# Gate and scale vectors of an output projection: other tiles, another queue, another order

## The chip, the cores and the metric

One core of a Trainium2 chip runs the whole program. The metric is the device time of one execution in microseconds. TensorE (PE) multiplies, with its own weight loads (PEld); VectorE (DVE), ScalarE (ACT) and GpSimd (POOL) do the elementwise work; SyncE (SP) issues nearly all DMAs. Each engine works through its own instructions in order.

## The reference

Two layers over 256 tokens `x` and 256 context tokens `xc`, model width 1024, float32. What matters here is the end of a layer's first half and the router that follows:

```python
merged = sigmoid(ga) * (y_a @ w_pa) + sigmoid(gb) * (y_b @ w_pb)
x = x + gt1 * (merged @ w_out)                    # gate gt1 per column
h2 = modulate(rmsnorm(x, g_ffn), sh2, sc2)        # h * (1 + sc2) + sh2
g_logits = h2 @ w_group + b_group                 # 4 groups
e_logits = h2 @ w_erouter + b_erouter             # 32 experts
# top group, top 2 experts in it, then per expert
y = (silu(h2 @ w1[e]) * (h2 @ w3[e])) @ w2[e]     # weighted, summed per token
x = x + gt2 * y
```

`gt1`, `sh2`, `sc2`, `gt2` are slices of 1024 columns of a vector of 6 * 1024 that the conditioning gives for each stream. The first layer updates both streams (512 tokens); the second, which is the last, updates only `x` (256 tokens).

## The kernel before

Each layer is a fixed order of stages: the input projections, spatial gating and retention, two projections that are merged, the output projection with the residual, the router, and 32 experts with 64 slots each. Matrix products outside the experts are made in three passes (`mm3`, lines 267 to 269) of high and low parts; `split_w` makes the parts of a weight piece on ACT (L209, `whi`) and DVE (L210, `wlo`).

**Weights.** `plan` lists the pieces of 512 KB in the order of use. `take` (L303) hands out the next and first fills a list of three with `fill`, so each piece is loaded two takes ahead. There are three buffers each for raw, high and low parts. `take` also calls `pump`, which loads expert weights ahead, in a ring of u4, a4, raw and high and low tiles. All these loads stand in SP's one queue in the order in which they are written; a load whose tile is not free holds up all behind it.

**Pools.** u4 has 30 tiles and a4 has 7, of 4 KB per partition; t2 has 7 of 2 KB. A new tile takes a buffer that its last readers have left. In the first layer, a4 also holds the vector that is being made for the next layer (`ada_steps`: raw tiles and an accumulator, read last by the matmuls of L448); in both it holds some weights of the first expert or two.

**Output projection.** `tok_wide` makes the first 512 columns for all token tiles (four in the first layer, two in the second) in four weight pieces of 256 rows. Then `residual(0)` and `residual(1)` follow for quarters of 256 columns: DVE multiplies by the gate (L980) and adds to the residual (L982), a third product with the scale gives `h2` (L984: POOL for the first three quarters, DVE for the last), and ACT squares for the norm (L986). `tok_major` makes the third quarter in two pieces, `(2, 0)` and `(2, 1)`, and `residual(2)` follows; `out_tile` makes the last quarter tile by tile, with `residual(3)` for each.

**Gate and scale vectors.** `mod_slices` loads, for a quarter and for each stream, both vectors to all partitions (256 KB into a t2 tile, L543). The first two quarters' slices are loaded on SP with weight pieces 2 and 3 (numbered from 0) of `tok_wide`, those of the last quarter with its second piece. Those of the third quarter are loaded by POOL's queue, in the program behind `residual(1)`.

**Router.** `route_piece(pc)` transposes `h2` of a quarter on PE (L993), ACT copies the result out of PSUM (L996), and a second step, `logits` (L1002), multiplies it by the router's weights. `defer(n, f)` puts `f` at the n-th next `tick`; `tok_major` has two ticks, one after each piece, and `flush()`, after `residual(2)`, runs what is left. So before, the transposes of piece 0 stand at the first tick, its logits at the second, and the transposes of piece 1, asked for at a third, run in `flush()`. The order of what follows is written out by hand (L1083): in `"o0 r o1 R t0 o2 ..."`, `o` is an `out_tile`, `r` the logits of piece 1 and the transposes of piece 2, `R` the logits of piece 2, `t` and `l` transposes and logits of the last quarter of a tile.

PE and SP run in program order throughout; from the second merging projection on, DVE, ACT and POOL do too.

Of the kernel before, what the change touches and what calls it, by code (L numbers as in the profile page):

```python
# [17 lines left out]
ALU = mybir.AluOpType  # L18
# [3 lines left out]
P = 128  # L22
# [32 lines left out]
def hybrid_kernel(  # L55
# [6 lines left out]
    nc = tc.nc  # L62
    depth = w_in.shape[0]
    V, S, G, T = nc.vector, nc.scalar, nc.gpsimd, nc.tensor
# [23 lines left out]
    def a4t(shape=(P, D), dt=F32):  # L88
        return a4.tile(list(shape), dt, tag="a4", name=nm("a4"))
# [45 lines left out]
    ada_d = [dr.tile([2, 6 * D], F32, name=f"ada{l}") for l in range(depth)]  # L135
# [89 lines left out]
    def defer(n, fn):  # L225
        deferred.append((ticks[0] + n, fn))
        deferred.sort(key=lambda d: d[0])
# [308 lines left out]

    ms = {}

    def mod_slices(l, pc, eng=None):
        r = []  # L540
        for i in range(1 if l == depth - 1 else 2):
            tl = t2t((P, 2, 256))
            (eng or nc.sync).dma_start(tl, ada_d[l][i].rearrange("(v n) -> v n", v=6)[2:5:2, pc * 256:(pc + 1) * 256].partition_broadcast(P))  # L543
            r.append(tl)
        return r

    def out_piece(l, pc, kh):
        r = piece(w_out[l], pc * 256, kh)
        if kh and pc == 3:
            ms[l, pc] = mod_slices(l, pc)  # L550
        return r

    def out_wide(l, q):
        r = piece_wide(w_out[l], 0, q)
        if q > 1:
            ms[l, q - 2] = mod_slices(l, q - 2)
        return r

    def plan(l):
# [15 lines left out]
    for l in range(depth):  # L575
        last = l == depth - 1
        layer[0], taken[0] = l, 0
        units.clear()
        nt = 2 if last else 4
# [117 lines left out]
        else:  # L697
# [9 lines left out]
            os_ = [bank() for _ in range(KD // 2)]  # L707
# [3 lines left out]
            for kp in range(KD // 2):  # L711
                if kp % 2 == 0:
                    tl = u4t((P, 4, NX))
# [40 lines left out]
        for g in range(2) if last else (1, 0):  # L754
            if last:
                os_, _ = tok_wide(tw)
            else:
                os_ = vo if g else [bank() for _ in tw]
# [3 lines left out]
                if not g:  # L762
                    for t in range(nt):
                        V.tensor_tensor(out=first[t], in0=os_[t], in1=first[t], op=ALU.add)
                    os_ = first
# [25 lines left out]
        for pc in range(4):  # L791
            os_, _ = feat_major(fj)
# [23 lines left out]
        for pc in range(4):  # L816
# [4 lines left out]
            os_, _ = feat_major(fj)  # L821
# [5 lines left out]
            os_, _ = feat_major([(f, yT, 0, nq) for f in range(2)])  # L827
            for f in range(2):
                if len(mg) * nq % 1024 == 0:
                    mgt = u4t((P, 1024 // nq, nq))  # L830
                m = mgt[:, len(mg) % (1024 // nq)]
# [6 lines left out]
        for h in range(HEADS):  # L838
# [10 lines left out]
            os_, _ = feat_major(qkj)  # L849
            qk = []  # L850
            for i in range(2):
                n = nq if i == 0 else NTOK
                o = os_[i]
                r = t2t()
# [60 lines left out]
            os_, _ = tok_wide(vgj)  # L915
# [9 lines left out]
        for pc in range(4):  # L925
            os_, gate_a_ = feat_major(fj)
# [16 lines left out]
        for pc in range(4):  # L943
            os_, gate_b = feat_major([(f, yT, 0, nq) for f in range(2)])
            m = [t2t() for _ in range(2)]
# [10 lines left out]
        res = []  # L956
# [10 lines left out]
        h2 = [u4t() for _ in range(nt)]  # L967
# [9 lines left out]
        def residual(pc, ts, os_, ms):  # L977
            cs = slice(pc * 256, (pc + 1) * 256)
            for t, o in zip(ts, os_):
                V.tensor_tensor(out=o, in0=o, in1=ms[t // 2][:, 0], op=ALU.mult)  # L980
            for t, o in zip(ts, os_):
                V.tensor_tensor(out=res[t][:, cs], in0=res[t][:, cs], in1=o, op=ALU.add)  # L982
            for t, o in zip(ts, os_):
                (G if pc < 3 else V).tensor_tensor(out=h2[t][:, cs], in0=res[t][:, cs], in1=ms[t // 2][:, 1], op=ALU.mult)  # L984
            for t, o in zip(ts, os_):
                S.activation(o, res[t][:, cs], AF.Square, accum_out=ssq[:, t, pc:pc + 1])  # L986

# [17 lines left out]
        def route_piece(pc):  # L1005
            rs_ = [turned(pc, (2 * i, 2 * i + 1)) for i in range(ns)]

            def rest():
                o = bank()
                for i in range(ns):  # L1010
                    logits(pc, (2 * i, 2 * i + 1), rs_[i], o)
                ov, lv = o[:, 0:nt * 36], lr[:, 0:nt].rearrange("p t e -> p (t e)")
                if pc == 0:
                    V.tensor_copy(lv, ov)
                else:
                    V.tensor_tensor(out=lv, in0=lv, in1=ov, op=ALU.add)

            return rest

        os_, _ = tok_wide([(mT[t // 2], t % 2 * P, 512) for t in range(nt)])  # L1020
        for pc in range(2):
            residual(pc, range(nt), [o[:, pc * 256:(pc + 1) * 256] for o in os_], ms[l, pc])
        ms[l, 2] = mod_slices(l, 2, G)
        waiting = []
        defer(1, lambda: waiting.append(route_piece(0)))
        defer(2, lambda: waiting.pop(0)())
        defer(3, lambda: waiting.append(route_piece(1)))
        os_, _ = tok_major([(mT[t // 2], t % 2 * P) for t in range(nt)])
        residual(2, range(nt), os_, ms[l, 2])
        wts = [take() for _ in range(2)]  # L1030
# [1 line left out]
        for i in range(ns):  # L1032
            tl = u4t()
# [49 lines left out]
        for op in ("o0 r o1 R t0 o2 l0 t1 s0 O3 l2 t3 s1 l3" if nt == 4 else "o0 r t0 o1 R l0 t1 l1").split():  # L1083
            t = int(op[1]) if op[1:] else None
# [20 lines left out]
        if split:  # L1105
            for t in range(nt):
# [7 lines left out]
                        in1=rc[:, 0:ns, None, :].to_broadcast([P, ns, 2, 36]), op=ALU.add)  # L1114
# [8 lines left out]
        for t in range(nt):  # L1123
# [5 lines left out]
                        in1=gf.to_broadcast([P, nt, GROUPS]), op=ALU.is_equal)  # L1129
# [3 lines left out]
                        in0=lo[:, 0:nt, 0:32].rearrange("p t (g e) -> p t g e", g=GROUPS),  # L1133
                        in1=goh[:, :, :, None].to_broadcast([P, nt, GROUPS, PER_GROUP]), op=ALU.add)
# [529 lines left out]
```

## Time and profile before

| | us |
|---|---|
| median of 3 runs | 1857.84 (1856.88 to 1861.28) |
| profiled execution | 1858.8 |
| its span, first to last instruction | 1857.0 |
| PE busy | 1798.0 (97%) |
| DVE busy | 916.7 (49%) |
| ACT busy | 590.9 (32%) |
| POOL busy | 386.3 (21%) |
| output projection and router, first layer | about 478 to 561 |
| experts, first layer | about 561 to 1047 |
| output projection and router, second layer | about 1332 to 1378 |
| experts, second layer | about 1378 to 1844 |

Times in the profile are microseconds from the start of the span. A row of the timeline gives start, length, engine, line, operation, names of output and inputs, and in brackets how long the engine sat idle before it and what released it. Rows of one kind that follow each other are merged, and their number stands at the end. A row of a table by stretch gives, per engine, busy time with the number of instructions, then the granted clock of TensorE as a share of 2.4 GHz, the share of the DMA engines' time, and GB/s.

### The profile page before, as it was taken

How to read it: one execution, taken by the hardware profiler on the slowest of the kernel's cores; microseconds unless marked ns; L12 is line 12 of the kernel's file. 1: busy time of each engine (PE TensorE's matmuls, PEld its weight loads, DVE VectorE, ACT ScalarE, POOL GpSimd, SP SyncE). 2: the span in 40 equal slices, each digit the busy share in tenths (PEclk: the TensorE clock that was granted, in tenths of full speed). 3: DMA queues.
4: the chain of work that ended last, by engine and by line, in shares of the span. 5: the costliest groups of instructions: out<-in, count | busy, mean ns of one | idle time of the engine just before them, and what ended most of it. 6: DMA issues, size and time to landing. Idle time of an engine off the chain costs nothing. (4 is left out here: it accounts for less than half of the span.)

```text
span 1857.0 us, 26227 instructions
## 1 busy us (share of the span) xinstructions
PE 1798.0 (97%) x9975; PEld 1190.8 (64%) x9975; DVE 916.7 (49%) x1582; ACT 590.9 (32%) x979; POOL 386.3 (21%) x351
## 2 busy tenths in 40 slices
PE   7999999999969999999999899999989999999996
PEld 4888888888865444454544489999964444444442
DVE  4878886664544323333332577767633222222223
ACT  4432345432332222121212364454432222221222
POOL 1021022100130424232323340211021212112111
PEclk9999999999979999999999999999989999999998
DMA  9546544454568999999999569656789999999996
GB/s 346 179 144 226 183 137 125 147 205 167 150 224 303 407 409 408 408 408 409 408 408 407 171 209 299 206 173 213 248 331 339 409 409 409 409 409 409 409 409 251
DMA packets 227893, 553.35 MB, mean 298 GB/s; under 512 B 23633, under 2 KB 105969, under 8 KB 227762
## 3 DMA queue, kind: packets, MB, share of 16 engines
q1 hardware_dynamic: 227138, 550.78, 79.6%
q8 instruction: 80, 1.31, 0.3%
q0 software_dynamic: 624, 0.84, 0.2%
q14 instruction: 51, 0.42, 0.1%
HBM read 550.45 MB, written 1.10 MB: 297 GB/s over the span
## 5 line engine op out<-in xcount | busy, mean ns | idle before, releaser
L1339 POOL TENSOR_TENSOR u<-u,t 128x512 f32<-128x512 f32 x184 | 230.5, 1287 | 723.1 <-DVE t L1338 723.1
L1297 PE MATMUL mm<-u,a 128*64 128x512 f32 x1376 | 334.6, 593 | 3.1 <-DMA u<-in_w_dram 1.8
L1324 DVE SCALAR_TENSOR_TENSOR a<-mm,sw,a 64x512 fp32r<-64x512 f32 x128 | 96.0, 750 | 356.8 <-ACT a L1323 356.0
L267 PE MATMUL mm<-u,whi 128*128 128x256 f32 (+1 forms) x800 | 269.9, 337 | 0.0
L269 PE MATMUL mm<-u,wlo 128*128 128x256 f32 (+1 forms) x800 | 267.9, 335 | 1.6 <-DVE wlo L210 1.6
L268 PE MATMUL mm<-u,whi 128*128 128x256 f32 (+1 forms) x800 | 267.7, 335 | 0.0
L210 DVE TENSOR_TENSOR wlo<-raw,whi 128x1024 fp32r<-128x1024 f32 x159 | 203.2, 1282 | 112.7 <-ACT whi L209 109.3
L209 ACT ACTIVATE whi<-raw 128x1024 fp32r<-128x1024 f32 x160 | 169.5, 1065 | 203.0 <-PE mm L268 82.3
L1297 PEld LDWEIGHTS mm<-u,a 128*64 128x64 f32 x1376 | 105.8, 137 | 198.9 <-issue 172.7
L267 PE MATMUL mm<-whi,u 128*128 128x512 f32 (+1 forms) x496 | 181.8, 366 | 2.0 <-ACT u L610 1.3
L268 PE MATMUL mm<-wlo,u 128*128 128x512 f32 (+1 forms) x496 | 178.9, 361 | 0.3 <-DVE wlo L210 0.3
L269 PE MATMUL mm<-whi,u 128*128 128x512 f32 (+1 forms) x496 | 178.7, 360 | 0.2 <-DVE u L612 0.2
L1301 DVE TENSOR_TENSOR t<-mm,t 64x512 f32<-64x512 f32 x64 | 43.7, 683 | 273.8 <-ACT t L1300 273.8
L1323 ACT ACTIVATE a<-mm,sw 64x512 fp32r<-64x512 f32 x128 | 87.4, 683 | 246.7 <-PE mm L1314 189.2
L269 PEld LDWEIGHTS mm<-u,wlo 128*128 128x128 f32 x800 | 152.1, 190 | 17.4 <-DVE wlo L210 2.2
L267 PEld LDWEIGHTS mm<-u,whi 128*128 128x128 f32 x800 | 152.3, 190 | 16.8 <-issue 1.2
L268 PEld LDWEIGHTS mm<-u,whi 128*128 128x128 f32 x800 | 152.4, 190 | 14.6
L1314 PE MATMUL mm<-u,t 128*64 128x512 f32 x664 | 155.4, 603 | 0.5 <-ACT t L1308 0.5
L1300 ACT ACTIVATE t<-mm 64x512 f32<-64x512 f32 x64 | 38.1, 595 | 297.3 <-PE mm L1297 297.3
L1338 DVE TENSOR_TENSOR t<-mm,u 128x512 f32<-128x512 f32 x190 | 118.6, 677 | 3.4 <-POOL u L1339 3.3
L267 PEld LDWEIGHTS mm<-whi,u 128*128 128x128 f32 x496 | 96.0, 194 | 19.7 <-issue 4.5
L269 PEld LDWEIGHTS mm<-whi,u 128*128 128x128 f32 x496 | 96.0, 193 | 14.1 <-DVE u L612 0.6
(311 smaller groups left out, 2471.8 us busy)
## 6 DMA issues: line engine op xcount, KB each, us to landing
u<-in_w_dram SPq DMA_DIRECT2D x510, 512.0 KB
raw<-in_w_dram SPq DMA_DIRECT2D x75, 512.0 KB
whi<-in_w_dram SPq DMA_DIRECT2D x73, 512.0 KB
wlo<-in_w_dram SPq DMA_DIRECT2D x73, 512.0 KB
raw<-in_w_in_dram SPq DMA_DIRECT2D x64, 512.0 KB
u<-in_w_ada_dram SPq DMA_DIRECT2D x49, 512.0 KB
raw<-in_w_in_dram SPq DMA_DIRECT2D x96, 256.0 KB
a<-in_w_ada_dram SPq DMA_DIRECT2D x47, 512.0 KB
```

The costliest lines, as they stand in the source:

```text
L209: S.activation(hi, rv, AF.Copy)
L210: low_by[0].tensor_tensor(out=lo, in0=rv, in1=hi.bitcast(F32), op=ALU.subtract)
L267: T.matmul(out, lhsT=sh, rhs=mh, start=first, stop=False)
L268: T.matmul(out, lhsT=sh, rhs=ml, start=False, stop=False)
L269: return T.matmul(out, lhsT=sl, rhs=mh, start=False, stop=last)
L1297: T.matmul(o[h * 64:(h + 1) * 64, :], lhsT=x[:, s0:s0 + 64], rhs=w(k), start=(k == 0), stop=(k == KD - 1), tile_position=(0, 64 * h))
L1301: V.tensor_tensor(out=hh[0:64], in0=o[0:64, :], in1=hh[0:64], op=ALU.mult)
L1314: T.matmul(o[n % banks][n * 64:(n + 1) * 64, :], lhsT=hTt[:, s], rhs=wc(s)[:, n * 512:(n + 1) * 512], start=(s == 0), stop=(s == 3), tile_ ...
L1323: S.activation(dh, src, AF.Copy, scale=w)
L1324: V.scalar_tensor_tensor(out=dl, in0=src, scalar=w, in1=dh.bitcast(F32), op0=ALU.mult, op1=ALU.subtract)
L1338: V.tensor_tensor(out=y, in0=o, in1=g2[t // 2][:, hs], op=ALU.mult)
L1339: eng.tensor_tensor(out=res[t][:, hs], in0=res[t][:, hs], in1=y, op=ALU.add)
```

## The change

The slices of the first two quarters are loaded at once: `mod_wide` loads both vectors for 512 columns into one a4 tile per stream (512 KB), with weight piece 2 of `tok_wide`, and `residual(0)` and `residual(1)` read halves of it. The slices of the third quarter are loaded on SP, with the second piece of its own weights, into t2 tiles as before; POOL issues none. L984 of the last layer runs on DVE for all quarters. The transposes of piece 1 are put into the same tick as the logits of piece 0, behind them; before, they ran in `flush()`, behind `residual(2)`.

```diff
@@ -536,24 +536,33 @@
-    def mod_slices(l, pc, eng=None):
+    def mod_wide(l):
+
+        r = []
+        for i in range(1 if l == depth - 1 else 2):
+            tl = a4t((P, 2, 512))
+            nc.sync.dma_start(tl, ada_d[l][i].rearrange("(v n) -> v n", v=6)[2:5:2, 0:512].partition_broadcast(P))
+            r.append(tl)
+        return r
+
+    def mod_slices(l, pc):
         r = []
         for i in range(1 if l == depth - 1 else 2):
             tl = t2t((P, 2, 256))
-            (eng or nc.sync).dma_start(tl, ada_d[l][i].rearrange("(v n) -> v n", v=6)[2:5:2, pc * 256:(pc + 1) * 256].partition_broadcast(P))
+            nc.sync.dma_start(tl, ada_d[l][i].rearrange("(v n) -> v n", v=6)[2:5:2, pc * 256:(pc + 1) * 256].partition_broadcast(P))
             r.append(tl)
         return r
 
     def out_piece(l, pc, kh):
         r = piece(w_out[l], pc * 256, kh)
-        if kh and pc == 3:
+        if kh:
             ms[l, pc] = mod_slices(l, pc)
         return r
 
     def out_wide(l, q):
         r = piece_wide(w_out[l], 0, q)
-        if q > 1:
-            ms[l, q - 2] = mod_slices(l, q - 2)
+        if q == 2:
+            ms[l, 0] = mod_wide(l)
         return r
@@ -981,7 +990,7 @@
             for t, o in zip(ts, os_):
-                (G if pc < 3 else V).tensor_tensor(out=h2[t][:, cs], in0=res[t][:, cs], in1=ms[t // 2][:, 1], op=ALU.mult)
+                (G if pc < 3 and not last else V).tensor_tensor(out=h2[t][:, cs], in0=res[t][:, cs], in1=ms[t // 2][:, 1], op=ALU.mult)
@@ -1019,12 +1028,10 @@
         os_, _ = tok_wide([(mT[t // 2], t % 2 * P, 512) for t in range(nt)])
         for pc in range(2):
-            residual(pc, range(nt), [o[:, pc * 256:(pc + 1) * 256] for o in os_], ms[l, pc])
-        ms[l, 2] = mod_slices(l, 2, G)
+            residual(pc, range(nt), [o[:, pc * 256:(pc + 1) * 256] for o in os_], [m[:, :, pc * 256:(pc + 1) * 256] for m in ms[l, 0]])
         waiting = []
         defer(1, lambda: waiting.append(route_piece(0)))
-        defer(2, lambda: waiting.pop(0)())
-        defer(3, lambda: waiting.append(route_piece(1)))
+        defer(2, lambda: (waiting.pop(0)(), waiting.append(route_piece(1))))
         os_, _ = tok_major([(mT[t // 2], t % 2 * P) for t in range(nt)])
         residual(2, range(nt), os_, ms[l, 2])
         wts = [take() for _ in range(2)]
```

## Rows read from the trace of the kernel before

**Rows 1.** PE's waits over the whole span: us in total, times, longest.

```profile
PE mm L1002 <- ACT t L996: 11.6, 5, 7.3
...
PE mm L1297 <- DMA u<-in_w_dram: 1.8, 3, 0.6
```

**Rows 2.** Timeline of the first layer, 515 to 526 us.

```profile
521.52 0.76 DVE L980 TENSOR_TENSOR mm<-mm,t 128x256 f32<-128x256 f32 x2 [2.83 <-DMA t<-ada]
...
522.69 2.96 POOL L984 TENSOR_TENSOR u<-u,t 128x256 f32<-128x256 f32 x4 [14.90 <-DVE u L982]
...
524.25 1.05 ACT L996 ACTIVATE t<-mm 128x512 f32<-128x512 f32 x2
```

**Rows 3.** Timeline of SP, ACT and POOL, first layer's output projection.

```profile
469.06 0.90 SPq L543 DMA_DIRECT2D t<-ada  x2
...
490.25 0.37 SPq L243 DMA_DIRECT2D raw<-in_w_out_dram  x1
503.55 1.77 SPq L543 DMA_DIRECT2D t<-ada  x2
...
482.47 1.06 ACT L209 ACTIVATE whi<-raw 128x1024 fp32r<-128x1024 f32 x1 [1.87 <-PE mm L269]
...
506.25 1.55 POOL L543 DMA_DIRECT2D t<-ada  x2
```

**Rows 4.** Line 543, all issues: time to landing of those from POOL.

```profile
DMA to landing us min/median/max: 7.6/11.7/14.4
```

**Rows 5.** Timeline of PE alone, first layer, 480 to 560 us.

```profile
487.75 0.64 PE L448 MATMUL mm<-a,ones 128*32 128x256 f32 x8
...
493.91 0.38 PE L469 MATMUL mm<-ident,t 128*128 128x128 f32 x2
...
511.97 1.87 PE L1002 MATMUL mm<-wr,t 128*128 128x36 f32 x16
513.68 1.07 PE L993 MATMUL mm<-ident,u 128*128 128x128 f32 x8
...
524.87 3.63 PE L1002 MATMUL mm<-wr,t 128*128 128x36 f32 x16 [7.25 <-ACT t L996]
...
534.24 1.87 PE L1002 MATMUL mm<-wr,t 128*128 128x36 f32 x16
```

**Rows 6.** Busy us by stretch, first layer: PE, PEld, DVE, ACT, POOL, PEclk, DMA.

```profile
505.00:518.00 13.00, 12.62 (x109) 12.41 (x107) 3.02 (x4) 2.99 (x4) 2.79 (x4) 1.00 0.82 213
...
526.00:528.00 2.00, 2.00 (x11) 2.00 (x11) 0.00 (x0) 0.00 (x0) 0.00 (x0) 0.50 0.93 369
```

**Rows 7.** Timeline of PE alone, second layer.

```profile
1347.95 0.44 PE L993 MATMUL mm<-ident,u 128*128 128x128 f32 x2 [1.50 <-POOL u L984]
...
1360.47 1.08 PE L1002 MATMUL mm<-wr,t 128*128 128x36 f32 x8 [2.87 <-ACT t L996]
...
1361.99 0.37 PE L267 MATMUL mm<-whi,u 128*128 128x256 f32 x1
...
1366.45 1.43 PE L1002 MATMUL mm<-wr,t 128*128 128x36 f32 x12
```

**Rows 8.** Busy us by stretch, second layer, columns as in rows 6.

```profile
1363.00:1365.00 2.00, 2.00 (x12) 2.00 (x11) 0.00 (x0) 0.00 (x0) 0.00 (x0) 0.50 1.03 410
```

**Rows 9.** SP's longest waits, first (600 to 700 us), then second expert stage (1500 to 1600).

```profile
SPq L296 <- PE mm L1314: 39.6, 24, 5.3
...
SPq L296 <- DMA u<-in_w_dram: 48.3, 54, 0.9
```

**Rows 10.** By stretch, second expert stage, columns as in rows 6.

```profile
1390.00:1395.00 5.00, 5.00 (x29) 2.54 (x30) 0.49 (x4) 0.98 (x2) 0.00 (x0) 1.00 0.20 82
...
1700.00:1800.00 100.00, 100.00 (x522) 47.05 (x520) 27.75 (x54) 21.75 (x38) 19.86 (x16) 1.00 1.03 409
```

**Rows 11.** Line 984 whole: duration ns min/median/max, first and last start, forms.

```profile
L984 POOL TENSOR_TENSOR u<-u,t x18: 716/732/909, 500.7 to 1359.8; 128x256 f32<-128x256 f32 x18
...
L984 DVE TENSOR_TENSOR u<-u,t x6: 424/424/636, 524.4 to 1367.6; 128x256 f32<-128x256 f32 x6
```

## Prediction

> **What bounds the kernel now.** I read three views in this order: the waits of TensorE over the whole span, the timeline around the largest of them, and the transfers around both expert stages.
>
> TensorE is busy for 97% of the span, so only a gap on it is worth anything. Its largest wait is one of L1002, the router's logits, for ACT's L996 [rows 1]. The timeline shows what stands behind it [rows 2]: L996 copies the transposed columns of piece 1 out of PSUM, and ACT works in order; ahead of L996 stand the squares of `residual(2)`; these need DVE's L982, this needs L980, and L980 waits for the gate slice of the third quarter. POOL issued that slice at 506.25 [rows 3], after all eight of its multiplications for the first half, because only then had buffers come free; it took up to 14.4 us to land [rows 4]. So PE stands still from 517.62 (524.87 less 7.25) [rows 5]. The idle time has a second price: before it the granted clock is 1.00 (2.4 GHz), after it 0.50 (1.2 GHz) [rows 6], and the work up to 534.24 runs at that level for the most part.
>
> The second layer has the same pattern, smaller: 1.50 us before the transposes of piece 0, which wait for POOL's L984, 2.87 us before the logits of piece 1, and then 0.50 of the clock [rows 7, 8].
>
> Does time gained in these stages reach the end? In the first expert stage SP waits mostly for buffers that PE must free [rows 9]: PE leads there, and whatever starts earlier ends earlier. In the second, SP waits mostly for transfers, they run at 409 GB/s [rows 9, 10], and PE has its first waits for expert weights at the very end [rows 1]: there the stream is level with PE. But at 1390 to 1395 the stream ran at 82 GB/s [rows 10], because the ring of buffers was full and PE had not freed any. That hole closes by as much as PE comes earlier.
>
> **The change, part by part.**
>
> *The slices of the first half* become tiles of pool a4 of 512 KB, loaded with weight piece 2: per layer and stream one transfer for two. Bytes are the same (12 slices of 256 KB before; 3 of 512 and 6 of 256 after). They start where the first of them started, 469.06 [rows 3], and are needed once PE is through weight piece 3, which it begins at 494.3 [rows 5]: no cost. They hold two of seven a4 buffers (one in the second layer). At that point I count four live ones in the first layer (two expert tiles, an accumulator, one raw tile) and six expert tiles in the second, so there is room, by one in the second layer. The transfer of weight piece 3 now has 512 KB more ahead of it: at the 409 GB/s of [rows 10] 1.3 us. Its split at 482.47 waited for PE, not for the transfer [rows 3], so that is covered; bare it would be 1.3 us per layer.
>
> *Four tiles leave pool t2.* Before, SP stopped between 490.25 and 503.55 at the slices of the last quarter, for want of a t2 tile [rows 3], with the scale rows and the expert weights queued behind. Now t2 holds four slices instead of eight, and I expect no stop. The weights then start some 13 us earlier; nothing on PE waits for them, so I price this at nothing, and it covers the earlier start of PE.
>
> *The slices of the third quarter* move from POOL to SP, behind weight piece (2, 1), which SP issues ahead of the row at 490.25. Even with the longest landing of POOL's, 14.4 us [rows 4], they are there at 505, while the columns they belong to leave PE at 511.97 [rows 5]. The wait for the transfer is gone.
>
> *The transposes of piece 1* are now recorded in the tick after the logits of piece 0, ahead of `residual(2)`. PE did them straight after those logits before, too (513.68), but ACT's copy now stands ahead of the squares. It can be done some 0.7 us after the last transpose (two copies take 1.05 [rows 2], the first beside the transposes), at 515.5. So the logits of piece 1 follow `out_tile(0)` at 517.62.
>
> What is late next? The transposes of piece 2 need `residual(2)` whole. The logits of piece 0 end at 513.84 [rows 5], DVE adds a copy of 0.3; four L980 (two in 0.76 [rows 2], starts 0.33 apart) end at 515.6; POOL starts 0.5 later and needs 2.96 for four [rows 2]: 519.1. PE reaches them after 16 logits, 1.71 (511.97 to 513.68), at 519.33. They fit by 0.2 us; at POOL's slowest, 0.91 each [rows 11], PE would wait 0.5. I take 0.1.
>
> First layer: the idle time 7.25, and the stretch from 524.87 to 534.24, 9.37 us, at full clock: logits 1.71, transposes 1.07, `out_tile` 2.87 (514.75 to 517.62), 5.65 together. That gives 7.25 + 3.72 - 0.1 = 10.9 us. Bounds: 7.0 if the clock falls all the same, 11.2 at most.
>
> *L984 of the second layer moves from POOL to DVE*: six of 0.42 us [rows 11], 2.5 us more on DVE, 0.73 us less of latency each. For piece 0, PE could begin with POOL's first product at 1347.95 [rows 7]. On DVE that product has to follow two L982 instead of one and is shorter by 0.3: I put it 0.2 earlier, the second 0.5 earlier. PE gains 0.5. Behind these on DVE stand `residual(1)` and two splits, later by some 0.8 us; their weights are needed 3 us later, so this costs nothing. DVE's L984 took up to 0.64 where POOL worked beside it; with POOL out of it I use the 0.42. The Trainium skill, GPSIMD Engine Reference, Specifications, says that GpSimd shares its SBUF interfaces with VectorE and contends with DVE instructions with two SBUF inputs; the row with 0.42 to 0.64 agrees with it. By that rule the second layer is freed of it, and the first, where POOL's four products still overlap with `residual(3)` of tile 0, keeps 0.2 us for each of its DVE steps, hidden behind 4 us of PE's work.
>
> Second layer: 0.5 from piece 0; 2.87 before the logits of piece 1, less a new wait: the transposes of the last quarter of tile 0 come 1.4 us after `out_tile(0)` (three DVE steps of 0.43 and their starts), PE has 0.8 + 0.4 us of logits and transposes meanwhile, so 0.2; and `out_tile(1)`, 1361.99 to 1366.45, 4.46 us at half clock, 2.87 at full: 1.6. Sum 4.8. Bounds: 2.5 (no clock back, 0.5 more waiting) and 6.7 (the clock does not fall after the 1.50 us either).
>
> Sum: 10.9 + 4.8 = 15.7 us. The profiled execution took 1858.8, its span is 1857.0, and the 1.8 around it stays. It stands 1.0 above the median of the runs, 1857.84; off the median, 1842.1 us.
>
> **Rivals.**
>
> *The second layer's gain stays in the weight stream* (1847). For it: the stream is at 409 GB/s from 1400 to the end, and PE waits for weights there 1.8 us [rows 1, 10]. Against it: the hole at 1390 to 1395 alone leaves 4 us of transfer time, and the stretch around it more; it is there because PE is late. If the stream's end were fixed, 10.9 would be left: 1857.84 - 10.9 = 1846.9.
>
> *The clock falls all the same* (1847). The stages keep short transposes and logits of 36 columns, and after only 1.50 us of idle time it fell in the second layer. Against it: from 505 to 518, with the same kinds of work and no gap, it is 1.00 [rows 6]. Without the clock's share (3.7 and 1.6): 10.4, so 1847.4.
>
> *It doesn't do what it says* (1855). SP may stop at the third quarter's slices as it did at the last quarter's, for a tile held until POOL's first products end. Issued at 503.55 they land at 515 to 518, so `residual(2)` and with it piece 2 stays late, and only the logits of piece 1 (1.7 us per layer at most) come forward: some 3 us. Against it: t2 holds four tiles fewer.
>
> *Slower*: SP stops at the wide tile itself, with weight pieces 3 and (2, 0) queued behind it. Piece 3, issued behind the slices of 469.06, was split at 482.47, so it needs at most 13.4 us to land, then 2.3 for the two parts of the split (1.06 on ACT, some 1.2 on DVE), and PE wants it at 494.3 [rows 3, 5]; so a stop until 478.6 is free, and each us after that costs at most one. The last reader of an a4 tile that is no expert weight is L448, done at 488.4 [rows 5]: 9.8 us, which still leaves a gain of 6. Slower by 0.3% it becomes from a stop until 499.9 (15.7 + 5.6 = 21.3 us after 478.6). Only an expert tile is held so long. That would come to 1864 or more.
>
> **How the numbers follow.** Changes under 0.3%, 5.6 us, can't be told from none here. Forecast 0.66; second layer's gain lost 0.13; clock falls all the same 0.11; no effect 0.05; slower 0.05. Faster by over 0.3% are the first three: 0.90. The forecast's own bounds go from 1857.84 - 11.2 - 6.7 = 1840 to about 1844; the two rivals reach 1847.4. I take 1838.5 to 1848.5, a margin of 1 us or so at either end for short stalls around these stages that I have not priced.
>
> **What would show it.** Right: no wait of L980 for a slice; no idle time between `out_tile(0)` and the logits of piece 1; a clock of 1.00 for the second `out_tile` of both layers; POOL without DMAs of slices; SP at the last quarter's slices near 491; the first expert matmul 11 us earlier in the first layer and 15 to 16 in the second; a shallower hole in the stream near 1380. Wrong: SP stopped at a slice or a wide tile; PE waiting for L984 before the transposes of piece 2; longer waits for expert weights at the end.

## The result, and the profile after

The changed kernel takes 1839.7 us (median of 4 runs, 1838.8 to 1840.9), the kernel before, run beside it, 1858.6 (median of 4, 1856.9 to 1861.3): ratio 0.990, 95% interval 0.9888 to 0.9911, some 19 us faster. The profiled executions took 1858.8 and 1838.8 us, their spans are 1857.0 and 1837.0.

Lines stand a few further down now: L980, L982, L984 and L986 are L989, L991, L993 and L995; L993 (transposes), L996 and L1002 are L1002, L1005 and L1011; L1297 is L1304; slices are loaded at L552, wide tiles at L544.

PE's waits over the whole span (us in total, times, longest), to be read against [rows 1]:

```profile
PE mm L1011 <- ACT t L1005: 1.5, 3, 0.5
PE mm L1002 <- DVE u L993: 1.5, 3, 1.1
...
PE mm L1304 <- DMA u<-in_w_dram: 1.2, 2, 0.6
```

The wait of 11.6 us is 1.5 now, and PE waits no longer for expert weights than before. The timeline of PE in the first layer, against [rows 5]:

```profile
510.76 1.87 PE L1011 MATMUL mm<-wr,t 128*128 128x36 f32 x16
512.46 1.07 PE L1002 MATMUL mm<-ident,u 128*128 128x128 f32 x8
...
516.25 1.87 PE L1011 MATMUL mm<-wr,t 128*128 128x36 f32 x16
517.95 1.07 PE L1002 MATMUL mm<-ident,u 128*128 128x128 f32 x8
...
521.74 1.87 PE L1011 MATMUL mm<-wr,t 128*128 128x36 f32 x16
```

No row here has a bracket: PE waits for nothing between them. From the logits of piece 0 to those of piece 1 it takes 5.49 us (before 12.90, with the idle time of 7.25), and from there to those of piece 2 another 5.49 (before 9.37). The other engines in the same stretch, against [rows 2, 3]:

```profile
467.71 0.93 SPq L544 DMA_DIRECT2D a<-ada  x2
...
481.08 1.33 SPq L552 DMA_DIRECT2D t<-ada  x2
...
489.45 2.07 SPq L552 DMA_DIRECT2D t<-ada  x2
...
512.89 1.42 DVE L989 TENSOR_TENSOR mm<-mm,t 128x256 f32<-128x256 f32 x4
513.13 1.09 ACT L1005 ACTIVATE t<-mm 128x512 f32<-128x512 f32 x2 [6.33 <-PE mm L1002]
...
514.70 2.81 POOL L993 TENSOR_TENSOR u<-u,t 128x256 f32<-128x256 f32 x4 [9.61 <-DVE u L991]
```

SP goes past the wide tiles, the third quarter's slices and the last quarter's (489.45; before, it stopped there until 503.55). The gate product of the third quarter begins at 512.89, behind DVE's copy of the logits of piece 0 and not behind a load; before, its parts waited for their slices, the last until 521.52 [rows 2]. POOL's four products end at 517.51, and PE comes for them at 517.95. By stretch (columns as in [rows 6]), the first layer and then the two places of the second that were slow:

```profile
505.00:518.00 13.00, 13.00 (x115) 13.00 (x114) 6.63 (x14) 5.11 (x15) 2.90 (x5) 1.00 0.81 308
518.00:535.00 17.00, 14.59 (x122) 13.92 (x121) 8.05 (x22) 5.07 (x13) 3.98 (x4) 1.00 0.41 144
1336.00:1340.00 4.00, 3.88 (x33) 3.67 (x32) 3.01 (x7) 3.12 (x7) 0.00 (x0) 1.00 0.96 317
1345.00:1348.00 3.00, 2.78 (x24) 2.81 (x25) 0.51 (x4) 1.03 (x4) 0.57 (x1) 1.00 1.03 410
```

The granted clock is 1.00 (2.4 GHz) in all four; before, it was 0.50 (1.2 GHz) in the stretches of [rows 6, 8]. PE in the second layer, against [rows 7]:

```profile
1335.51 0.77 PE L1002 MATMUL mm<-ident,u 128*128 128x128 f32 x4 [0.21 <-DVE u L993]
...
1339.27 1.08 PE L1011 MATMUL mm<-wr,t 128*128 128x36 f32 x8
...
1343.53 0.98 PE L1011 MATMUL mm<-wr,t 128*128 128x36 f32 x8
...
1348.34 1.43 PE L1011 MATMUL mm<-wr,t 128*128 128x36 f32 x12
```

**Where the time came from.** I take two stretches, each between the same two events on PE. First layer, from the logits of piece 0 to the first expert matmul: 511.97 to 561.17 before, 510.76 to 548.26 after, 49.20 and 37.50 us, so 11.7 gained. Second layer, from the first transposes of piece 0 to the first expert matmul: 1347.95 to 1378.51, and 1335.51 to 1359.50, 30.56 and 23.99, so 6.57, and ahead of it the idle time went from 1.50 to 0.21, 1.29 more: 7.9. Together 19.6 of the 20.0 between the spans. What is left are 1.2 us gained ahead of the changed stage, 1.8 lost between the layers and 1.0 gained in the last experts. Code ahead of the first stretch is the same but for SP's loads, and in the twelve runs below it begins anywhere from 509.8 to 513.1, and the time between the two layers' stretches is anything from 785.0 to 787.4 (785.3 before, 787.0 after); I count the first two as the scatter of executions.

### The profile page after: what moved, and what is told of

Its sections match the earlier page's. It is cut to its first block, busy times and chain, and to the rows that moved or that the text cites. A ratio compares the mean times of both kernels' runs of the same rounds, so it can differ in the third digit from the quotient of the medians.

```text
span 1837.0 us, 26207 instructions
## 1 busy us (share of the span) xinstructions
PE 1789.0 (97%) x9975; PEld 1181.5 (64%) x9975; DVE 917.7 (50%) x1588; ACT 590.6 (32%) x979; POOL 378.5 (21%) x342
## 5 line engine op out<-in xcount | busy, mean ns | idle before, releaser
L1304 PE MATMUL mm<-u,a 128*64 128x512 f32 x1376 | 334.5, 593 | 3.4 <-ACT a L1219 1.4
L1304 PEld LDWEIGHTS mm<-u,a 128*64 128x64 f32 x1376 | 105.9, 137 | 198.9 <-issue 172.7
L268 PEld LDWEIGHTS mm<-u,whi 128*128 128x128 f32 x800 | 152.1, 190 | 14.4
```

The costliest lines, as they stand in the source:

```text
L268: T.matmul(out, lhsT=sh, rhs=ml, start=False, stop=False)
L1304: T.matmul(o[h * 64:(h + 1) * 64, :], lhsT=x[:, s0:s0 + 64], rhs=w(k), start=(k == 0), stop=(k == KD - 1), tile_position=(0, 64 * h))
```

## The experiments

Twelve kernels ran, each timed against the kernel before on the same chip; the kernel before took 1857.8 to 1859.0 in these rounds, which the ratios allow for and the medians do not. The two stretches are as above; the last column is PE's idle time ahead of the second layer's transposes of piece 0 (a dash: none in the trace).

| run | us | ratio, 95% interval | first layer | second layer | idle |
|---|---|---|---|---|---|
| before | 1858.6 | | 49.20 | 30.56 | 1.50 |
| changed kernel | 1839.7 | 0.990 (0.9888 to 0.9911) | 37.50 | 23.99 | 0.21 |
| before + order | 1851.8 | 0.9966 (0.9954 to 0.9978) | 45.43 | 27.34 | 1.59 |
| before + wide tiles | 1851.4 | 0.9958 (0.9945 to 0.9972) | 43.32 | 31.33 | 0.30 |
| before + third quarter on SP | 1842.8 | 0.9913 (0.9900 to 0.9927) | 38.35 | 24.09 | 1.49 |
| changed, old order | 1839.6 | 0.9901 (0.9886 to 0.9917) | 38.27 | 24.22 | - |
| changed, products on POOL | 1838.9 | 0.9896 (0.9881 to 0.9911) | 37.51 | 23.95 | - |
| changed, both of these | 1839.1 | 0.9897 (0.9881 to 0.9914) | 38.69 | 24.80 | - |
| changed, third quarter by POOL | 1839.4 | 0.9899 (0.9884 to 0.9914) | 38.85 | 24.78 | - |
| the same, products on POOL | 1846.0 | 0.9932 (0.9915 to 0.9948) | 38.96 | 30.99 | 0.65 |
| changed, narrow loads | 1840.8 | 0.9903 (0.9888 to 0.9918) | 37.51 | 24.01 | 1.37 |
| changed in the first layer alone | 1848.1 | 0.9937 (0.9923 to 0.9950) | 37.52 | 31.36 | 1.25 |
| before, waits filled with matmuls | 1854.2 | 0.9974 (0.9965 to 0.9984) | 46.42 | 30.85 | 1.65 |
| changed, wait ahead of the experts filled | 1838.3 | 0.9890 (0.9873 to 0.9906) | 37.97 | 24.22 | - |

**The order alone, on the kernel before.**

```diff
-        defer(2, lambda: waiting.pop(0)())
-        defer(3, lambda: waiting.append(route_piece(1)))
+        defer(2, lambda: (waiting.pop(0)(), waiting.append(route_piece(1))))
```

> The kernel before with the new order alone: the transposes of piece 1 in the tick of the logits of piece 0, slices, queues and products as before. Theory A (the slices of the third quarter come too late, the order only decides who stands behind them): in the first layer the logits of piece 1 start at once behind the first out_tile, about 517.6 us instead of 524.9, but then the transposes of piece 2 wait for residual(2), whose gate product still starts near 521.5 and whose scale products on POOL end near 525.7; so the idle time moves one step on and shrinks by some 3 us, and the clock falls all the same. In the second layer 2.9 us of waiting go and 0.5 to 1.5 come back before piece 2 or the last quarter. Time 1851 to 1855. Theory B (the order was the fault: ACT's copies stood behind the squares): the idle time of both layers is gone or under 2 us, 1841 to 1845.

PE in the first layer:

```profile
518.00 1.87 PE L1002 MATMUL mm<-wr,t 128*128 128x36 f32 x16
523.83 2.06 PE L993 MATMUL mm<-ident,u 128*128 128x128 f32 x6 [3.96 <-POOL u L984]
```

The logits of piece 1 no longer wait, but the next thing that needs `residual(2)` does: 3.96 of the 7.25 us are there again, one step later, and the clock is 0.50 from 524 to 531. 1851.8, as theory A has it.

**The order undone, on the changed kernel** (the diff above reversed).

> The changed kernel with the old order: the transposes of piece 1 again run behind residual(2), all else as changed. Theory A (early slices): residual(2) has its slices in time, so the squares of four tiles end near 517.2 and the copies of piece 1 near 518.2 in the first layer; PE, done with the first out_tile at 516.25, waits about 1.7 us; in the second layer the copy is there before PE comes. 1841 to 1842; up to 1845 if 1.7 us of idle time cost the clock as the 1.50 us did in the second layer before. Theory B (the order): the wait for the copies comes back whole, 1848 or more.

1839.6: no loss to be seen, less than either theory expected. The wait is 0.50 us in the first layer (my 1.7 had the squares of `residual(2)` ending 1 us later than they do) and 0.34 in the second. So the order helps where slices are late, and does next to nothing once they are early.

**The products of the last layer on POOL again** (`G if pc < 3 and not last else V` back to `G if pc < 3 else V`).

> The changed kernel with the scale products of the last layer's first three quarters back on POOL. Theory A1 (piece 0 came sooner because its weights' successor landed sooner, so that residual(0) starts earlier; the engine of the product matters little): the first product on POOL is there about 0.2 us later than on DVE, the second 0.7 later; PE loses 0.4 to 0.6 us, the clock stays 1.00, 1840 to 1840.5. Theory A2 (the product on DVE took away the idle time of 1.50 us before piece 0, and with it the fall of the clock): an idle time of over 1 us comes back before the transposes of piece 0, the clock falls to 0.50 behind it, 1842 to 1844.

1838.9, below both ranges. The transposes of piece 0 show no idle time ahead of them, and 0.25 between the tiles; the stretch behind is 23.95 us against 23.99. Theory A2 falls: moving the products to DVE took nothing away that is measured here.

**The third quarter's slices on POOL's queue again.**

```diff
-        if kh:
+        if kh and pc == 3:
             ms[l, pc] = mod_slices(l, pc)
...
+        ms[l, 2] = mod_slices(l, 2, G)
```

> The changed kernel with the third quarter's slices loaded by POOL's queue behind residual(1) again; wide tiles, order and products as changed. Theory A (late issue is what cost the time): issued near 505 us they land near 516 to 520 in the first layer; the transposes of piece 2 wait 4 to 6.5 us from 518 on, the clock falls and takes 3 to 4 more; in the second layer 3.5 us of waiting and 1.5 to 2 of clock: 1851 to 1855. Theory B (the order): the slices may come late, the time is within 3 us of the changed kernel, 1840 to 1843.

1839.4, just below theory B's range, and my theory A fell with it. POOL issued in the first layer at 505.40, as late as before (506.25), yet the slices were there sooner. Timeline of POOL, DVE and PE:

```profile
505.40 1.56 POOL L552 DMA_DIRECT2D t<-ada  x2
...
516.11 0.76 DVE L989 TENSOR_TENSOR mm<-mm,t 128x256 f32<-128x256 f32 x2 [2.09 <-DMA t<-ada]
...
519.43 0.44 PE L1002 MATMUL mm<-ident,u 128*128 128x128 f32 x2 [0.25 <-POOL u L993]
520.30 0.44 PE L1002 MATMUL mm<-ident,u 128*128 128x128 f32 x2 [0.43 <-POOL u L993]
```

They took 6.6 to 9.9 us to land, not up to 14.4 [rows 4], so PE waited 0.7 us there, and the first stretch is 1.35 us longer than in the changed kernel. In the second layer this run told nothing: with the products on DVE, POOL had nothing ahead of the issue and made it at 1306.5, some 35 us ahead of its use (1341.20). Two runs follow from that.

**The wide tiles alone, on the kernel before** (`mod_wide`, and `residual` for the first half reading from it; slices of the third quarter on POOL, order and products as before).

> The kernel before with the wide tiles alone: first half's vectors in a4, everything else as before (third quarter's slices on POOL's queue, order and products as before). Theory C, formed on the run of the changed kernel with POOL's queue put back: the wide tiles matter most, since with four t2 tiles free SP no longer stops at the last quarter's slices until 503.5 us, and so its burst of slices, scale rows and expert weights no longer runs beside POOL's slices; these land in 7 to 10 us instead of 14.4. In the first layer residual(2) then starts near 513 to 516, the logits of piece 1 wait about 3 us behind the squares, with some clock lost: 4 to 8 of the 11.5 us are gained. In the second layer the third quarter's slices are as late as before against PE (behind POOL's products), so its 2.9 us of waiting stay, but the next weight piece lands sooner: 1 to 3 us gained. 1847 to 1853. Theory A (late issue by POOL is the whole of it): POOL still issues near 505, so at most 2 us are gained, 1855 or more.

1851.4, in the range of theory C. POOL issues at 506.00, no sooner than before, and its slices take, min/median/max:

```profile
DMA to landing us min/median/max: 6.6/8.2/9.8
```

What they met on the way is seen by stretch, first in the kernel before (the DMA share and GB/s are the last two numbers):

```profile
503.00:508.00 5.00, 5.00 (x44) 5.00 (x44) 2.59 (x5) 4.68 (x12) 4.79 (x7) 1.00 0.23 60
508.00:512.00 4.00, 4.00 (x36) 4.00 (x35) 1.23 (x1) 0.02 (x1) 0.00 (x0) 1.00 0.94 115
```

and in the changed kernel with the slices on POOL's queue, where SP does not stop either:

```profile
503.00:508.00 5.00, 5.00 (x44) 5.00 (x44) 2.55 (x4) 4.14 (x10) 3.96 (x6) 1.00 1.03 412
508.00:512.00 4.00, 4.00 (x37) 4.00 (x35) 0.43 (x1) 0.00 (x0) 0.00 (x0) 1.00 1.03 288
```

In the kernel before, the DMA engines were nearly idle while SP stood still (0.14 of their time from 490.5 to 503.5); then the last quarter's slices, the scale rows, expert weights and POOL's slices were issued within a few us, and the engines were full (0.94) at only 115 GB/s. Without the stop SP has issued slices and scale rows by 492.4, and POOL's slices meet mostly weights: the engines are just as full, but move 412 and 288 GB/s in the two rows above (413 and 301 with the wide tiles alone). So full engines alone don't make the landing late. That the other vectors under way held POOL's slices up fits the runs, but no run moved these vectors alone.

With four t2 tiles free SP does not stop, and the wait for the copies behind the squares is 2.60 us instead of 7.25, the clock falling behind it all the same (0.62 from 519 to 528): 5.9 us gained in the first stretch. In the second layer the wait stayed (5.00 us, PE being there sooner), and with it the stretch of 31.33 us; less idle time ahead of it leaves 0.4 us gained, not the 1 to 3 expected.

**The same queue, with the products of the last layer on POOL** (both edits above on the changed kernel).

> The run with the slices on POOL's queue again, now with the scale products of the last layer on POOL too, as before, so that in the second layer as well POOL issues the third quarter's slices only behind residual(1) (in the earlier run POOL had no products left there and issued the slice 30 us ahead of its use). Theory: in the first layer under 1 us is lost, as in the earlier run; in the second the slice is issued near 1338.5 and lands near 1345 to 1347, 4 to 5 us after PE could use it, and the new order can't hide that: PE waits 3 to 5 us before the transposes of piece 2 and the clock may fall behind it: 1843 to 1846.5. Rival (the order alone makes up for a late slice in the second layer too): 1839 to 1841.

1846.0. Now POOL issues behind its products in the second layer too. Timeline of POOL and PE there:

```profile
1338.08 0.81 POOL L552 DMA_DIRECT2D t<-ada  x1
...
1348.55 1.80 PE L1002 MATMUL mm<-ident,u 128*128 128x128 f32 x6 [3.83 <-POOL u L993]
...
1354.79 1.42 PE L1011 MATMUL mm<-wr,t 128*128 128x36 f32 x12
```

3.83 us of waiting, the clock 0.50 behind it (from 1348 to 1354), 7.0 us in the stretch and some 6 in the time. With wide tiles and new order the first layer can bear slices from POOL, the second can't.

**The third quarter's slices on SP alone, on the kernel before** (`if kh and pc == 3:` to `if kh:`, and the load on POOL taken out).

> The kernel before with the third quarter's slices on SP alone, behind the second piece of their weights; narrow slices in t2, order and products as before. The rival of the prediction (it doesn't do what it says) put to the test: SP stops for a t2 tile at the third quarter's slices, until the first products on POOL end near 501 to 503.5 us. Theory C: the slices then stand first behind the stop and land within 7 to 10 us, at 509 to 513, just in time; the first layer gains nearly all of its 11 us less 0.5 to 2 for the old order; in the second layer, where SP stops likewise for one tile until about 1348, they land near 1355, 1 us or 2 sooner than before: 1844 to 1849. The rival: the stop keeps them late, they land at 515 to 518 with the expert weights behind them late as well, 1852 or more.

1842.8, faster than either theory expected: this one move gives 16 of the 19 us. SP in the first layer:

```profile
481.91 7.03 SPq L543 DMA_DIRECT2D t<-ada  x2
...
503.15 1.77 SPq L543 DMA_DIRECT2D t<-ada  x2
```

SP stops at the third quarter's slices as well, but only for 4.9 us (for a tile that DVE's L452 still uses, not for POOL's products), and is past them by 488.9, 14 us ahead of where I had the end of the stop; it stops at the last quarter's, until 503.15, as before. That stop costs PE nothing that is seen here: the first stretch is 38.35 us, and 38.27 with the old order on the changed kernel, which has no such stop. The wait for the copies is 0.50 us, as with the old order on the changed kernel.

**Order and products both undone, on the changed kernel**: only the places and queues of the slices are left of the change.

> The changed kernel with both the order and the products undone: only the wide tiles and the third quarter's slices on SP are left of the change. Theory D, from the runs so far: the slices are the whole of the change, order and products are worth 0.5 us or less each because residual(2) is now early enough for either: 1839.3 to 1841. Rival: each of the two hides the loss of the other, and without both a wait of 1 to 3 us comes back before the logits of piece 1 in the second layer: 1842 to 1845.

1839.1, theory D. PE in the second layer:

```profile
1335.53 0.44 PE L1002 MATMUL mm<-ident,u 128*128 128x128 f32 x2
1336.22 0.44 PE L1002 MATMUL mm<-ident,u 128*128 128x128 f32 x2 [0.25 <-POOL u L993]
...
1343.63 1.08 PE L1011 MATMUL mm<-wr,t 128*128 128x36 f32 x8
```

Neither wait comes back, so the two were not hiding each other's loss. Its second stretch, 24.80 us, is 0.8 longer for another reason (the last section).

**Narrow loads into the wide tiles** (256 columns with weight piece 2, 256 with piece 3).

> The changed kernel with each wide a4 tile filled by two loads of 256 columns instead of one of 512: the first with weight piece 2, the second with piece 3, as the slices were loaded before. Theory C2 (in the second layer the wide load takes 256 KB out of the way of weight piece (2, 1), which lands 1.1 us sooner against PE, so that residual(0) starts sooner, PE's 1.50 us before the transposes of piece 0 are gone and with them a fall of the clock): the piece is late again, 1 to 1.5 us of idle time come back there, the clock falls to 0.50 behind it: 1841.5 to 1843.5. Theory C3 (the number and time of the loads do not matter, the freed t2 tiles do): as the changed kernel, 1839 to 1840.3.

1840.8, between the two ranges. The idle time ahead of the second layer's piece 0 is back at 1.37 us, the clock did not fall behind it (3.77 us to the logits, 3.76 in the changed kernel). Its trace and the table's last column say the same: with 512 columns in one load 0 to 0.65 us, with 256 in each 1.25 to 1.65. The medians differ by 1.1 us, which the intervals alone would not tell from nothing.

**The second layer as before, the first as changed.**

> The changed kernel with all four parts undone in the second layer alone. Theory A: the layers add up; the first layer's 11.3 to 11.7 us of the profile reach the end whole, the second layer's part of 6 to 8 is missing: 1845.5 to 1847. If the second layer's part of the gain were given by the weight stream instead (PE's waits for weights at the end), the time would be 1843 or less; if the first layer's gain were lost in the stages between, 1849 or more.

1848.1, 1 us above the range: by the medians the first layer is worth 10.9 us and the second some 8.4 of the time, by the ratios 11.7 and 6.9. What the second layer gains is not kept back by the weight stream.

**The waits of the kernel before filled with matmuls of no use** (`keep_busy(9 if last else 26)` ahead of the logits of piece 1).

> The kernel before with matrix work of no use put on PE ahead of the logits of piece 1, 52 matmuls of 0.12 us in the first layer (6.2 of the 7.25 us of waiting) and 18 in the second (2.2 of 2.87 us); nothing else changed, so that the slices, the squares and the copies come as late as before. Theory (the forecast's split of the gain: the wait itself and the clock that falls behind it are two terms, and the second hangs on PE standing still): the logits of piece 1 start no sooner, but the stretch up to the logits of piece 2 runs at 1.00 and takes 5.5 to 5.7 us instead of 9.37 in the first layer, with 1 to 2 us more in the second: 1852.5 to 1854. Rival (the clock falls for the short transposes and logits, whatever stood before them): no gain, 1857.5 to 1859.

PE in the first layer:

```profile
516.75 5.96 PE L237 MATMUL mm<-iota,ident 128*128 128x128 f32 x52
523.97 1.98 PE L1002 MATMUL mm<-wr,t 128*128 128x36 f32 x16 [1.25 <-ACT t L996]
...
531.13 1.87 PE L1002 MATMUL mm<-wr,t 128*128 128x36 f32 x16
```

In the first layer the slices came as late as before, and still 4.2 us are gained (by the ratio 4.8): from the logits of piece 1 to those of piece 2 it takes 7.16 us instead of 9.37. That is 2.2 of the 3.9 that the clock costs there, less than expected; with 1.25 us of idle time left the mean clock is still 0.81 from 526 to 535. The whole first stretch is 2.8 us shorter. The second layer gained nothing (30.85 us against 30.56): its slice came 1 us later than before, and 2.00 us of idle time were left. So some 2 us of the 4.2 lie outside both stretches, and what gives them stays open. The wait and the clock are two terms, as the forecast had them; the rival, that short matmuls bring the clock down whatever stood before them, falls in part here and in full in the changed kernel, where the same matmuls run at 1.00 with no idle time ahead.

**The wait ahead of the first layer's experts filled** (`keep_busy(20)` there, `keep_busy(3)` behind the counts).

> The changed kernel with matrix work of no use put into the 5.50 us for which PE waits ahead of the first layer's experts (40 matmuls of 0.12 us), and 6 more behind the counts, as the second layer has them. Theory E1 (a low clock costs only where PE sets the end): the 32 matmuls of L1358 run at full clock and end 1.5 to 1.9 us sooner, but the first expert matmul waits for ACT's L1362, which stands behind the exponentials of the gate and did not wait for PE: 0 to 0.4 us gained, 1839 to 1840. Theory E2: what the clock takes there reaches the end: 1.5 to 2 us gained, 1837.5 to 1838.3.

1838.3, at the end of E2's range, but the intervals of its ratio and the changed kernel's overlap, and its first stretch is no shorter (37.97 us). The 32 matmuls (L1356 there) run at full clock, but wait 0.74 us for DVE, and the first expert matmul still waits for ACT's copies. By the trace E1 holds for this stage; the time alone can't decide between the two, and I know of no cause in the stage for the 1.4 us between the medians. No run here beats the changed kernel by more than its interval.

## Why the prediction was right, and where its terms were off

The forecast was 1842.1 us, the measurement 1839.7, inside the range of 1838.5 to 1848.5; the likeliest case came about. By its steps:

**What bounds the kernel.** Right: the wait of [rows 1] went, and the time with it. The first layer's 10.9 us are 11.7 in the profile: 7.41 up to the logits of piece 1 (forecast 7.25), 3.88 up to those of piece 2 (3.72), and 0.41 behind, where I had nothing; the wait of 0.1 for POOL didn't come, PE being 0.44 us behind it.

**The third quarter's slices.** Right, and the larger part of the change. My reason for the lateness was half of it: to the late issue came what SP issued all at once when its stop ended. I took the 14.4 us of [rows 4] as what a load from POOL takes; with SP not stopped it was 10 at most. And POOL did not issue late because buffers came free only then: with wide tiles and free t2 tiles it issued as late (505.40 and 506.00), right behind its own products.

**The order.** The prediction has the copy ahead of the squares as what lets the logits of piece 1 start. Once the slices are early it is worth 0.50 and 0.34 us of waiting, not to be seen in the time.

**The wide tiles.** No cost, as priced: SP passes them at 467.71 without a stop. With the third quarter's slices on SP, the stop at the last quarter's costs PE nothing, also as priced (third quarter on SP alone); with them on POOL's queue it went with their late landing. But I gave them no gain, and there is one of 1.2 us in the second layer. Against PE's last matmul ahead of piece 0, ACT's split of weight piece (2, 1) begins 2.4 us before it in the kernel before (1343.72 and 1346.16) and 3.5 in the changed one (1331.48 and 1335.02). It waits for that load in both, and DVE's part of it stands ahead of `residual(0)`. The run with narrow loads puts just these 256 KB back behind weight piece 3: the split begins 2.4 us before PE's last matmul again, and the idle time comes back. How much of the time this is worth is less clear: third quarter on SP alone and the changed kernel without order and products differ by the wide tiles alone, and are 3.0 us apart by their ratios, with intervals that overlap; 1.5 us of it are this idle time.

**The second layer, the term that was mis-sized**: 4.8 forecast with an upper bound of 6.7, 7.9 measured in the profile.

| step | forecast | measured |
|---|---|---|
| idle time ahead of piece 0 | 0.5 | 1.29 |
| transposes of piece 0 to its logits (5.34 to 3.76 us) | 0 | 1.58 |
| to the logits of piece 1 (7.18 to 4.26) | 2.67 | 2.92 |
| `out_tile(1)`, to the last logits but one (5.98 to 4.81) | 1.6 | 1.17 |
| from there to the first expert matmul (12.06 to 11.16) | 0 | 0.90 |

Two mistakes are in it. The 0.5 us ahead of piece 0 were credited to the products on DVE; they are worth nothing measurable, and the time came from the wide load, so that this part of the sum came true by luck. And 1.58 us of clock behind the idle time of 1.50 stood only in the upper bound, since I let this idle time shrink to 1.0 and the clock fall all the same. This cost is not in every execution: in the run with the second layer as before, the idle time was 1.25 us and the clock stayed at 1.00.

Nor is the last row the change's own. With the second layer as before, the same part takes 11.27 us in the run that changes the first layer alone, and 11.95 to 12.01 in four others with the wide tiles; it follows the clock of 30 matmuls that the last section shows at either level. Without it the second layer gained 7.0 us, still above the bound of 6.7.

The 0.2 us that each DVE step of the first layer was to keep beside POOL did not show as I put it. In the run with the slices on POOL's queue, L993, which has both inputs in SBUF, takes 0.64 us beside POOL's products, but L989 and L991, which read one input from PSUM, take 0.43 and 0.42; in the changed kernel L993 comes as POOL ends and takes 0.42 to 0.43. The Trainium skill, GPSIMD Engine Reference, Specifications, names DVE instructions with two SBUF inputs as those that contend, and the trace agrees with it. It bore on no term.

**The rivals.** The weight stream kept nothing back: the hole in it is still there (130 GB/s from 1375 to 1380, against the 82 of [rows 10]), PE's waits for weights fell from 1.8 to 1.2 us, and undoing the second layer alone costs 7 to 8. "The clock falls all the same" is refuted by the windows above, for the places that it named. "It doesn't do what it says" failed twice, SP getting a tile for the slices in time even without the wide ones. The slower case needed a stop at the wide tile; there was none.

## What to carry to other kernels

When a load comes late, look at what else its DMA engines were given in the same microseconds: here loads from POOL's queue took up to 14.4 us beside what SP issued all at once after a stop, and 10 at most where SP had not stopped. Issue a small vector on the queue of the work that needs it, behind that work's own weights, rather than on an engine that must first finish its arithmetic. Of a change in four parts undo each alone and do each alone: here one move did 16 of 19 us, two of the four parts could be left out, and single gains of 6, 7.5 and 16 us do not add up, since they shorten the same wait.

## What the runs showed of the hardware that was not expected

The DMA engines were full at few bytes where, by SP's and POOL's queues, mostly loads to all partitions were under way: 0.94 of their time for 115 GB/s (508 to 512 us, kernel before), against 1.03 for 409 in the last experts [rows 10]. With the third quarter on SP alone, so without POOL's loads, it was 1.01 for 164 GB/s in the same microseconds.

The clock did not follow the idle time just before as simply as the forecast had it. Ahead of the second layer's piece 0 it stayed at 1.00 behind idle times of 1.25, 1.37 and 1.49 us (narrow loads or slices), and fell behind 1.50, 1.59 and 1.65. But 1.49 and 1.50 are as good as equal, and in the first layer of the run with filled waits it fell behind 1.25, so the length of the idle time alone does not decide it. The 30 matmuls behind the last logits of that layer took 3.59 us in the changed kernel and 5.19 to 5.22 in three other runs (the changed kernel with slices on POOL's queue, with both order and products undone, and with the wait ahead of the experts filled), with the same 0.47 us of idle time ahead of those last logits in all four. By stretch, the changed kernel and then the one with both order and products undone:

```profile
1351.00:1354.00 3.00, 3.00 (x28) 3.00 (x29) 2.13 (x14) 2.98 (x3) 2.13 (x2) 1.00 1.03 410
```

```profile
1351.00:1354.00 3.00, 3.00 (x17) 3.00 (x18) 2.09 (x14) 2.98 (x3) 2.04 (x1) 0.59 1.03 411
```

PE is busy for all of both, and the clock is 1.00 in the one and 0.59 in the other. That costs some 0.8 us of the second layer's stretch in each of those three; what decides it stays open.
